# An encoder layer's last stage: finished output rows kept on chip and stored in four pieces per token tile, instead of three quarters parked in DRAM

## The chip, the cores and the metric

The kernel runs on one core of one Trainium2 chip. The metric is the device time of one execution in microseconds (us); less is better. The engines meant below are TensorE (PE in the profile, with its weight loads as PEld), VectorE (DVE), ScalarE (ACT), GpSimd (POOL) and SyncE (SP), whose queue issues nearly all transfers of this kernel.

## The reference

One encoder layer is applied to 512 + 256 = 768 tokens of width 2048. Only its end matters here:

```python
def mixer_layer(x, norm_g, w_in, conv_w, a_log, dt_bias, dn_gain, w_out):
    h = rms_norm(x, norm_g)
    proj = jnp.einsum('bsd,dp->bsp', h, w_in.astype(h.dtype)).astype(f32)
    ...
    mixed = jnp.concatenate([attn, dn], axis=-1).astype(x.dtype)
    return x + jnp.einsum('bsm,md->bsd', mixed, w_out.astype(x.dtype))

def encoder(...):
    x = mixer_layer(...)
    return rms_norm(x, final_norm_gain)     # y * rsqrt(mean(y*y) + eps) * gain, over all 2048 columns of a token
```

The final norm needs the sum of squares of a whole token row (2048 columns) before any column of it can be finished.

## The kernel before, in words

Everything is float32 in and out; each float32 operand of a product is split into a high and a low part, and three matmuls (high by high, high by low, low by high) make one product step. The projections, the attention heads and the DeltaNet heads come first; the mixed features (`mixD`) and several intermediates lie in DRAM.

The output projection is the last stage. It runs in two parts: part 0 takes the eight DeltaNet heads' features, part 1 the eight attention heads'. The features of part 0 are held in the tiles `xh0..xh7` and `xl0..xl7` of the pool `xp` (high and low part of one head, 128 x 768); those of part 1 in tiles `mh`/`ml` of the last pool `op`. Within a part the 2048 output columns are done in four quarters n = 0..3 of 512 columns (NQ = 4), and in a quarter the tokens in six tiles t = 0..5 of 128 (NT = 6). One token tile of one quarter is 8 heads x 3 = 24 matmuls of 512 columns into one PSUM bank `mmo`. (Where n is 0 the first three tiles are interleaved.) During the last token tile of a quarter `o_split` makes the weights of the next quarter: a load `st` of `w_out` arrives in one of five staging buffers, ACT casts the high part (`oh`), DVE or POOL subtracts (`ol`), and the buffer goes to a later load. These use the tiles `xh8..xh15`, `xl8..xl15`.

What is done with a finished bank is in three helpers. `o_fetch` asks for the other addend, a 128 x 512 tile `res` out of a ring of six (`wtile`): columns of `x` in part 0, the stored partial sum `yD` in part 1. `o_post` is called from `between` during the matmuls of the next token tile: DVE adds bank and `res`; in part 1 ACT then squares the sum with a running row sum (`sums`), and the sum is multiplied by the gain `fg` (on POOL in quarters 0 to 2, on DVE in quarter 3). `o_store` is called a little later and stores.

In part 1 the sums of quarters 0, 1 and 2 go from `res` to a DRAM buffer `zD`. In quarter 3 `o_fetch` also reads them back, into two tiles `row[0]` (columns 0 to 1023) and `row[1]` (1024 to 1535, its second half filled by the last quarter); the tag `row` has four buffers of 4 KB per partition, so two token tiles fit. After the last quarter's sum DVE and POOL make the row factor `r`, ACT multiplies `row[0]` by it and DVE `row[1]`, and both go to the output `y` as two 512 KB stores.

The order of instructions on each engine is the order in which the program is written; `drv` (a planner with costs) only decides where side tasks are woven in. All transfers named above are issued by SP in the order of the program: an issue that has to wait holds up all issues behind it. A buffer's next transfer waits until its earlier one is over.

Of the kernel before, what the change touches and what calls it, by code (L numbers as in the profile page):

```python
# [6 lines left out]
F32 = mybir.dt.float32  # L7
F32R = mybir.dt.float32r
AF = mybir.ActivationFunctionType
ALU = mybir.AluOpType  # L10
# [3 lines left out]
P = 128  # L14
D = 2048
NK = 16
T = 768
TP, TS = 512, 256
NT = T // P
# [48 lines left out]
class Driver:  # L68
# [88 lines left out]
    def spawn(self, gen, prio=0, bulk=False):  # L157
        self.n += 1
        self.tasks.append([self.end, prio, self.n, gen, bulk, None])
# [98 lines left out]
def encoder_kernel(tc, x, xT, wt, wab, wo, convw, gain, dngain, fgain, alog, dtb, cst, tabs, y):  # L258
# [3 lines left out]
    V, A, G = (Engine(drv, n, e) for n, e in (("V", nc.vector), ("A", nc.scalar), ("G", nc.gpsimd)))  # L262
    SY = DQ = Queue(drv, "Q", nc.sync)
    AQ = Queue(drv, "Q2", nc.scalar)
# [31 lines left out]
    yD = tc.dram_tile([NT, P, D], F32, name="yD")  # L296
    qD, kD, vD, agD = (tc.dram_tile([NH, P, T], F32, name=n) for n in ("qD", "kD", "vD", "agD"))
    gD = tc.dram_tile([NH, P, T], F32, name="gD")
    bD = tc.dram_tile([NK // 2, 2, P, HALF], F32, name="bD")
    zD = tc.dram_tile([NT, P, D], F32, name="zD")  # L300

    with (
        tc.manual_schedule(),
# [12 lines left out]
        def wtile(name):  # L316
            return drv.placed("w", wp.tile([P, 512], F32R, tag="w", name=name, bufs=6), 6)
# [29 lines left out]
        KB = 256  # L347
        TAGS, pool = {}, [None]

        def set_pool(p, tags):  # L350

            assert not any(drv.live.get(t, 0) for t in TAGS), drv.live
            pool[0] = p
            TAGS.clear()
            TAGS.update(tags)
            drv.most.update({t: n for t, (_, n) in TAGS.items()}, sa=2, sb=2, mm=4)
            for t in TAGS:
                drv.past.pop(t, None)
# [6 lines left out]
        if True:  # L365
            def st(tag, shape, name, dt=F32):

                n, bufs = TAGS[tag]
                t = drv.placed(tag, pool[0].tile([P, n], dt, tag=tag, name=name, bufs=bufs), bufs)
                v = t[:, :int(np.prod(shape))]  # L370
                if len(shape) == 2:
                    v = v.rearrange("p (a b) -> p a b", a=shape[0])
                elif len(shape) == 3:
                    v = v.rearrange("p (a b c) -> p a b c", a=shape[0], b=shape[1])
                return v
# [632 lines left out]
            def small(shape, tag, name, bufs=2):  # L1008
                return drv.placed(tag, pool[0].tile([P, *shape], F32, tag=tag, name=name, bufs=bufs), bufs)
# [515 lines left out]
            NQ = D // 512  # L1525
# [84 lines left out]
            def m_second():  # L1610
                for j in range(NH):
                    hi, lo = (pool[0].tile([P, T], F32R, name=f"m{w}{j}") for w in "hl")
                    mset[1][j] = (hi, lo)
                    SY.dma_start(lo.bitcast(F32), mixD[j])
                for j in range(NH):
                    yield lambda: drv.ready(mset[1][j][1])
                    m_split(1, j)
                    yield "early"
# [43 lines left out]
            late, outs, gains = {}, {}, {}  # L1662

            def open_last():

                global_close()
                op = op_cm.__enter__()
                set_pool(op, dict(row=(4 * KB, 4), fg=(2 * KB, 2)))
                late["sums"] = op.tile([P, NT, NQ], F32, name="sums")
                late["mhalf"] = op.tile([P, 1], F32, name="mhalf")  # L1670
                V.memset(late["mhalf"], -0.5)
                spawn(m_second(), -1)
                for n in (0, 1):
                    o_gain(n)
# [3 lines left out]
            def global_close():  # L1678
                give(*(t for t in list(TAGS) for _ in range(drv.live.get(t, 0))))
                heads[0].__exit__(None, None, None)  # L1680

            def o_gain(n):
                gains[n] = st("fg", (512,), f"fg{n}")
                SY.dma_start(gains[n], fgain[n * 512:(n + 1) * 512].partition_broadcast(P))

            def o_fetch(part, n, t):

                c = slice(n * 512, (n + 1) * 512)
                res = wtile(f"res{part}{n}_{t}").bitcast(F32)
                SY.dma_start(res, x[t * P:(t + 1) * P, c] if part == 0 else yD[t][:, c])  # L1690
                row = None
                if part and n == NQ - 1:
                    row = [st("row", (2, 512), f"row{t}_{h}") for h in (0, 1)]
                    SY.dma_start(row[0], zD[t][:, :1024].rearrange("p (a b) -> p a b", a=2))
                    SY.dma_start(row[1][:, 0], zD[t][:, 1024:1536])
                outs[part, n, t] = (res, row)

            def o_post(ps, part, n, t):
                res, row = outs[part, n, t]
                if part == 0:  # L1700
                    V.tensor_tensor(out=res, in0=ps, in1=res, op=ALU.add)
                    return
                yt = row[1][:, 1] if row else res
                V.tensor_tensor(out=yt, in0=ps, in1=res, op=ALU.add)
                A.activation(ps, yt, AF.Square, accum_out=late["sums"][:, t, n:n + 1])
                (V if row else G).tensor_tensor(out=yt, in0=yt, in1=gains[n], op=ALU.mult)
                if not row:
                    return
                r = small([2], "r", f"r{t}")
                V.tensor_reduce(out=r[:, 0:1], in_=late["sums"][:, t], axis=AX.X, op=ALU.add)  # L1710
                V.tensor_scalar(out=r[:, 0:1], in0=r[:, 0:1], scalar1=1.0 / D, scalar2=EPS, op0=ALU.mult, op1=ALU.add)
                G.tensor_tensor(out=r[:, 1:2], in0=r[:, 0:1], in1=late["mhalf"], op=ALU.pow)
                A.mul(row[0], row[0], r[:, 1:2])
                V.tensor_scalar(out=row[1], in0=row[1], scalar1=r[:, 1:2], scalar2=None, op0=ALU.mult)

            def o_store(part, n, t):
                res, row = outs.pop((part, n, t))
                if not row:
                    SY.dma_start((zD if part else yD)[t][:, n * 512:(n + 1) * 512], res)
                    return  # L1720
                for h in (1, 0):
                    SY.dma_start(y[t * P:(t + 1) * P, h * 1024:(h + 1) * 1024].rearrange("p (a b) -> p a b", a=2), row[h])

            pend, done = [], []

            def between(i):

# [7 lines left out]
            for part in (0, 1):  # L1735
                for n in range(NQ):
                    if part and not late:
                        drv.drain()
                        open_last()
# [3 lines left out]
                    if n == 0:  # L1743

                        group = 3
                        drv.until(lambda: free("mm", group))
                        ps3 = [bank(f"o{part}_{t}") for t in range(group)]
                        for j in range(NH):
                            drv.until(lambda: j in mdone[part] and wmade[0] > NH * NQ * part + j)
                            for t in range(group):  # L1750
                                ostep(ps3[t], part, t, j)
                                drv.slot()
                            between(j)
                        while pend:
                            between(1)
                            between(3)
                        o_fetch(part, 0, 0)
                        for t in range(group):
                            if t:
                                o_fetch(part, 0, t)  # L1760
                            pend.append((ps3[t], part, 0, t))
                    for t in range(group, NT):
                        if not late and not drv.tasks:
                            open_last()
                        ps = bank(f"o{part}{n}_{t}")
                        o_fetch(part, n, t)
                        for j in range(NH):
                            ostep(ps, part, t, j)
                            between(j)
                            if t == NT - 1 and j and (part, n) != (1, NQ - 1):  # L1770
                                o_split()
                            drv.slot()
                        if t == NT - 1 and (part, n) != (1, NQ - 1):
                            o_split()
                        pend.append((ps, part, n, t))
# [43 lines left out]
```

## Time and profile before

| | us |
|---|---|
| median of 3 runs | 1657.13 (1653.51 to 1657.84) |
| profiled execution, own time | 1661.15 |
| its span in the trace | 1659.4 |
| PE busy in the span | 1597.8 (96%) |
| mean granted TensorE clock | 0.985 of 2.4 GHz |

Times of rows are us from the start of the span. The profiled execution took 4.0 us longer than the median run, and 1.75 us of it lie outside the span. The profile's slices show PE at 0.9 or more in nearly all of the span, and at 0.5 in the last fortieth; that last stretch is where the rows below are from. A row of the timeline gives start, duration, engine (SPq is SP's queue), source line, operation, written and read tile, number of instructions merged, and in brackets how long the engine had been idle and who ended that.

### The profile page before, as it was taken

To read this page: it belongs to the slowest core of one execution; us is meant where nothing else is said; L and a number is where in the kernel's file an instruction comes from. 1 tells how busy PE (TensorE), PEld (TensorE's weight loads), DVE (VectorE), ACT (ScalarE), POOL (GpSimd) and SP (SyncE) were. 2 spreads that over 40 slices of the span, in tenths; PEclk is the share of its full clock that TensorE was granted. 3 is DMA by queue.
4 is the path that set the end of the run, shared out by engine and by line. 5 is a ranking of instruction groups with operands and counts; after the bars stand their busy time and mean duration, and the time that the engine had idled before them with its cause. 6 is when DMAs were issued, how large, how long until landed. Compare 5 with 4: busy or idle time off the path is not lost.

```text
span 1659.4 us, 30160 instructions
## 1 busy us (share of the span) xinstructions
PE 1597.8 (96%) x11675; PEld 1411.5 (85%) x11675; DVE 934.0 (56%) x2003; ACT 799.6 (48%) x1800; POOL 237.2 (14%) x233
## 2 busy tenths in 40 slices
PE   7998999999999999999999999999999889999995
PEld 6887999999888898988888888888878678887874
DVE  6558877778445554556555555665355555444332
ACT  6655333434354565556455656545355554433322
POOL 0000000000222221222213121312110011111220
PEclk9998999999999999999999999999999899999998
DMA  6232232323423323222223332232335455646557
GB/s 244 80 122 86 99 105 94 110 89 116 164 83 91 83 71 94 79 78 92 78 67 92 100 80 75 77 84 91 102 125 178 149 172 172 194 137 225 156 171 276
DMA packets 135265, 198.51 MB, mean 120 GB/s; under 512 B 49393, under 2 KB 60241, under 8 KB 135121
## 3 DMA queue, kind: packets, MB, share of 16 engines
q1 hardware_dynamic: 133968, 193.43, 36.2%
q10 hardware_dynamic: 1152, 3.15, 0.5%
q8 instruction: 92, 1.51, 0.4%
q14 instruction: 53, 0.43, 0.1%
HBM read 150.08 MB, written 46.45 MB: 118 GB/s over the span
## 4 chain that ended last, share of the span: by engine, by line
PE 80%; DMA 6%; DVE 5%; issue 4%; ACT 3%; POOL 1%; SPq 1%; ACTq 0%; DVEq 0%; POOLq 0%
PE mm L286 36%; PE mmo L286 8%; PE mmY L286 7%; PE mmr L286 7%; PE c L286 5%; PE mmX L286 5%; PE mmZ L286 5%; PE m L286 2%; DMA out_y<-row 2%; DMA st<-in_wo 1%; PE kk L286 1%; PE o L286 1%; DMA ak<-kD 1%; PE S L286 1%; DMA res<-in_x 1%
## 5 line engine op out<-in xcount | busy, mean ns | idle before, releaser
L286 PE MATMUL mm<-xl_x,hip 128*128 128x512 f32 (+1 forms) x1152 | 307.2, 348 | 0.0
L286 PE MATMUL mm<-xh_x,lop 128*128 128x512 f32 (+1 forms) x1152 | 305.5, 346 | 0.0
L286 PE MATMUL mm<-xh_x,hip 128*128 128x512 f32 (+1 forms) x1152 | 304.5, 345 | 0.0
L204 ACT CAST hip<-st 128x512 fp32r<-128x512 f32 x244 | 150.9, 619 | 236.8 <-PE mm L286 74.2
L204 POOL TENSOR_TENSOR lop<-st,hip 128x512 fp32r<-128x512 f32 x72 | 97.3, 1351 | 928.4 <-ACT hip L204 826.3
L204 DVE TENSOR_TENSOR lop<-st,hip 128x512 fp32r<-128x512 f32 x172 | 120.9, 703 | 193.8 <-ACT hip L204 188.6
L286 PEld LDWEIGHTS mm<-xh_x,hip 128*128 128x128 f32 x1152 | 176.5, 189 | 22.8
L286 PEld LDWEIGHTS mm<-xh_x,lop 128*128 128x128 f32 x1152 | 176.6, 189 | 21.7
L286 PEld LDWEIGHTS mm<-xl_x,hip 128*128 128x128 f32 x1152 | 176.4, 189 | 21.2
L286 PE MATMUL mmr<-xh_x,raw 128*128 128x512 f32 (+1 forms) x512 | 118.5, 345 | 11.3 <-ACT xh_x L204 9.6
L204 DVE SCALAR_TENSOR_TENSOR cacc<-cin,cw,cacc 128x772 f32<-128x772 f32 x96 | 107.4, 1119 | 23.4 <-ACT cacc L204 22.0
L204 ACT ACTIVATE s<-s,m 128x512 f32<-128x512 f32 (+1 forms) x96 | 61.5, 648 | 97.5 <-DVE m L204 97.4
L286 PEld LDWEIGHTS mmr<-xh_x,raw 128*128 128x128 f32 x512 | 79.7, 191 | 25.3 <-ACT xh_x L204 9.9
L286 PE MATMUL mmo<-oh,xh_m 128*128 128x512 f32 x192 | 79.2, 412 | 4.6 <-DVE q L204 4.1
L286 PE MATMUL mmo<-oh,mh 128*128 128x512 f32 x192 | 76.6, 399 | 1.8 <-ACT mh L204 1.6
L286 PE MATMUL mmo<-ol,xh_m 128*128 128x512 f32 x192 | 76.8, 400 | 1.0 <-POOL ol L204 0.5
L286 PE MATMUL mmo<-ol,mh 128*128 128x512 f32 x192 | 76.6, 399 | 0.6 <-DVE ol L204 0.5
L286 PE MATMUL mmo<-oh,ml 128*128 128x512 f32 x192 | 76.6, 399 | 0.3 <-DVE ml L204 0.3
L286 PE MATMUL mmo<-oh,xl_m 128*128 128x512 f32 x192 | 76.2, 397 | 0.0
L286 PE MATMUL mmr<-xl_x,raw 128*128 128x512 f32 (+1 forms) x256 | 67.0, 343 | 0.4 <-DVE xl_x L204 0.4
L204 ACT ACTIVATE z<-c,rho 128x128 f32<-128x128 f32 x96 | 35.1, 367 | 66.6 <-PE c L286 66.5
L204 DVE TENSOR_TENSOR res<-mmo,res 128x512 f32<-128x512 f32 x42 | 28.8, 687 | 67.5 <-PE mmo L286 46.3
(256 smaller groups left out, 3287.0 us busy)
## 6 DMA issues: line engine op xcount, KB each, us to landing
st<-in_wt SPq DMA_DIRECT2D x256, 256.0 KB
st<-in_wo SPq DMA_DIRECT2D x64, 256.0 KB
dec<-gcD SPq DMA_DIRECT2D x24, 256.0 KB
res<-in_x SPq DMA_DIRECT2D x24, 256.0 KB
yD<-res SPq DMA_DIRECT2D x24, 256.0 KB
res<-yD SPq DMA_DIRECT2D x24, 256.0 KB
out_y<-row SPq DMA_DIRECT2D x12, 512.0 KB
xst<-in_xT SPq DMA_DIRECT2D x15, 384.0 KB
```

Source lines behind the costliest of these rows:

```text
L204: r = f(*a, **k)
L286: r = PE.matmul(out, lhsT, rhs, start=start, stop=stop, skip_group_check=more)
```

## The change

The buffer `zD` is gone. In part 1 the sum of quarter n < 3 and token tile t is written by DVE not over `res` but to a place of its own, number i = 6n + t. The places 0 to 15 are the sixteen tiles `xh0`, `xl0`, `xh1`, ... `xl7` (their first 512 columns), which held the features of part 0; places 16 and 17 are tiles of the tag `row`, now two buffers of 2 KB. ACT squares it there and POOL multiplies it by the gain there. Nothing of it is stored until quarter 3, whose own sum stays in `res`. When the row factor of a token tile is there, ACT multiplies the pieces of quarters 0 and 2 and DVE those of quarters 1 and 3, and the four pieces go out as four stores of 256 KB, the third on ACT's queue, the others on SP's.

```diff
-    zD = tc.dram_tile([NT, P, D], F32, name="zD")
...
-                set_pool(op, dict(row=(4 * KB, 4), fg=(2 * KB, 2)))
+                set_pool(op, dict(row=(2 * KB, 2), fg=(2 * KB, 2)))
...
                 SY.dma_start(res, x[t * P:(t + 1) * P, c] if part == 0 else yD[t][:, c])
-                row = None
-                if part and n == NQ - 1:
-                    row = [st("row", (2, 512), f"row{t}_{h}") for h in (0, 1)]
-                    SY.dma_start(row[0], zD[t][:, :1024].rearrange("p (a b) -> p a b", a=2))
-                    SY.dma_start(row[1][:, 0], zD[t][:, 1024:1536])
-                outs[part, n, t] = (res, row)
+                dst = res
+                if part and n < NQ - 1:
+
+                    i = n * NT + t
+                    dst = st("row", (512,), f"row{i}")
+                    if i < NK:
+                        dst = xp.tile([P, T], F32R, tag=f"x{'hl'[i % 2]}{i // 2}", name=f"row{i}")[:, :512].bitcast(F32)
+                    kept[n, t] = dst
+                outs[part, n, t] = (res, dst)
...
-                yt = row[1][:, 1] if row else res
                 V.tensor_tensor(out=yt, in0=ps, in1=res, op=ALU.add)
                 A.activation(ps, yt, AF.Square, accum_out=late["sums"][:, t, n:n + 1])
-                (V if row else G).tensor_tensor(out=yt, in0=yt, in1=gains[n], op=ALU.mult)
-                if not row:
+                (G if n < NQ - 1 else V).tensor_tensor(out=yt, in0=yt, in1=gains[n], op=ALU.mult)
+                if n < NQ - 1:
                     return
...
-                A.mul(row[0], row[0], r[:, 1:2])
-                V.tensor_scalar(out=row[1], in0=row[1], scalar1=r[:, 1:2], scalar2=None, op0=ALU.mult)
+                kept[n, t] = yt
+                for i in range(NQ):
+                    if i % 2:
+                        V.tensor_scalar(out=kept[i, t], in0=kept[i, t], scalar1=r[:, 1:2], scalar2=None, op0=ALU.mult)
+                    else:
+                        A.mul(kept[i, t], kept[i, t], r[:, 1:2])
...
-                res, row = outs.pop((part, n, t))
-                if not row:
-                    SY.dma_start((zD if part else yD)[t][:, n * 512:(n + 1) * 512], res)
-                    return
-                for h in (1, 0):
-                    SY.dma_start(y[t * P:(t + 1) * P, h * 1024:(h + 1) * 1024].rearrange("p (a b) -> p a b", a=2), row[h])
+                res, _ = outs.pop((part, n, t))
+                if part == 0:
+                    SY.dma_start(yD[t][:, n * 512:(n + 1) * 512], res)
+                elif n == NQ - 1:
+                    for i in range(NQ):
+                        (AQ if i == 2 else SY).dma_start(y[t * P:(t + 1) * P, i * 512:(i + 1) * 512], kept.pop((i, t)))
```

The order of PE's instructions is the same in both programs. SP issues 24 transfers fewer (18 stores to `zD`, 12 loads from it, 12 stores to `out_y` go; 18 stores to `out_y` come), and ACT issues six more.

SP's queue at the end of the program before (names are `res13_4` for part 1, quarter 3, tile 4, and `row4_0`, `row4_1` for the two halves of tile 4's row):

```order
L248 DMA res13_4_17027<-yD_58 128x512
L248 DMA row4_0_17029<-zD_65 128x1024
L248 DMA row4_1_17030<-zD_65 128x512
L248 DMA out_y<-row3_1_16988 128x1024
L248 DMA out_y<-row3_0_16987 128x1024
L248 DMA res13_5_17069<-yD_58 128x512
L248 DMA row5_0_17071<-zD_65 128x1024
L248 DMA row5_1_17072<-zD_65 128x512
L248 DMA out_y<-row4_1_17030 128x1024
L248 DMA out_y<-row4_0_17029 128x1024
L248 DMA out_y<-row5_1_17072 128x1024
L248 DMA out_y<-row5_0_17071 128x1024
```

The same place in the changed program (`row3`, `row9` are the kept pieces of tile 3 from quarters 0 and 1; the piece of quarter 2 is on ACT's queue):

```order
L248 DMA out_y<-row2_16258 128x512
L248 DMA out_y<-row8_16477 128x512
L248 DMA out_y<-res13_2_16954 128x512
L248 DMA res13_4_17038<-yD_58 128x512
L248 DMA out_y<-row3_16263 128x512
L248 DMA out_y<-row9_16509 128x512
L248 DMA out_y<-res13_3_16996 128x512
L248 DMA res13_5_17080<-yD_58 128x512
L248 DMA out_y<-row4_16298 128x512
L248 DMA out_y<-row10_16541 128x512
L248 DMA out_y<-res13_4_17038 128x512
L248 DMA out_y<-row5_16333 128x512
```

No load of a row stands between a tile's stores and the next ones any more; the load `res13_5` still stands behind the stores of tile 3.

SP's queue where the weights of quarter 2 are loaded (`st309` to `st316`), before:

```order
L248 DMA zD_65<-res11_3_16497 128x512
L248 DMA res11_5_16559<-yD_58 128x512
L248 DMA st309_16574<-in_wo 128x512
L248 DMA st310_16583<-in_wo 128x512
L248 DMA zD_65<-res11_4_16528 128x512
L248 DMA st311_16593<-in_wo 128x512
L248 DMA st312_16602<-in_wo 128x512
```

And in the changed program:

```order
L248 DMA res11_4_16538<-yD_58 128x512
L248 DMA res11_5_16570<-yD_58 128x512
L248 DMA st309_16587<-in_wo 128x512
L248 DMA st310_16596<-in_wo 128x512
L248 DMA st311_16605<-in_wo 128x512
L248 DMA st312_16614<-in_wo 128x512
```

The store to `zD` between the second and the third weight load is gone; the quarters before and after this one show the same.

DVE's last instructions before, for token tile 5:

```order
L204 TENSOR_TENSOR row5_1_17072<-mmo13_5_17068,res13_5_17069 128x512
L204 TENSOR_TENSOR row5_1_17072<-row5_1_17072,fg3_16863 128x512
L204 TENSOR_REDUCE r5_17113<-sums_16018 128x1
L204 TENSOR_SCALAR r5_17113<-r5_17113 128x1
L204 TENSOR_SCALAR row5_1_17072<-row5_1_17072,r5_17113 128x1024
```

And in the changed program:

```order
L204 TENSOR_TENSOR res13_5_17080<-mmo13_5_17079,res13_5_17080 128x512
L204 TENSOR_TENSOR res13_5_17080<-res13_5_17080,fg3_16879 128x512
L204 TENSOR_REDUCE r5_17124<-sums_16017 128x1
L204 TENSOR_SCALAR r5_17124<-r5_17124 128x1
L204 TENSOR_SCALAR row11_16573<-row11_16573,r5_17124 128x512
L204 TENSOR_SCALAR res13_5_17080<-res13_5_17080,r5_17124 128x512
```

The chain from the bank to the row factor is the same; the product over 1024 columns has become two of 512, and ACT's likewise.

## Rows read from the trace of the kernel before

**Rows 1.** The page's first line, and two stretches of the last 60 us.

```profile
span 1659.4 us, 30160 instructions
...
1600.00:1640.00 40.00, 39.78 (x171) 31.69 (x170) 16.65 (x30) 13.42 (x24) 4.79 (x6) 1.00 0.71 241
1640.00:1659.40 19.40, 1.70 (x8) 1.03 (x6) 4.72 (x10) 3.74 (x6) 1.08 (x2) 0.60 0.74 262
```

**Rows 2.** The chain that ended last, from 1595 us: shares, and its longest pieces.

```profile
by line: DMA out_y<-row 41.4%; PE mmo L286 10.8%; DMA res<-yD 9.2%; DMA row<-zD 8.3%; issue 5.1%; SPq L248 4.7%; DVE row L204 4.6%; DVE ol L204 2.5%; ACT mmo L204 1.1%; DVE res L204 1.1%; ACT oh L204 1.0%; POOL r L204 0.9%; DVE r L204 0.4%;
...
1618.39 7.59 DMA out_y<-row
...
1648.02 5.36 DMA row<-zD
```

**Rows 3.** Timeline of SP's queue, last tiles.

```profile
1634.18 0.76 SPq L248 DMA_DIRECT2D res<-yD  x1
1639.82 1.57 SPq L248 DMA_DIRECT2D row<-zD  x2
1641.50 0.84 SPq L248 DMA_DIRECT2D out_y<-row  x2
1642.39 0.98 SPq L248 DMA_DIRECT2D res<-yD  x1
```

**Rows 4.** Timeline of PE at the three quarter boundaries, and PE's last matmul.

```profile
1543.98 0.40 PE L286 MATMUL mmo<-oh,mh 128*128 128x512 f32 x1
...
1544.84 0.39 PE L286 MATMUL mmo<-oh,ml 128*128 128x512 f32 x1
...
1577.60 0.39 PE L286 MATMUL mmo<-oh,ml 128*128 128x512 f32 x1
...
1578.89 0.51 PE L286 MATMUL mmo<-ol,mh 128*128 128x512 f32 x1 [0.23 <-DVE ol L204]
1579.23 0.39 PE L286 MATMUL mmo<-oh,ml 128*128 128x512 f32 x1
...
1612.00 0.40 PE L286 MATMUL mmo<-oh,ml 128*128 128x512 f32 x1
...
1613.30 0.40 PE L286 MATMUL mmo<-oh,ml 128*128 128x512 f32 x1
...
1641.30 0.40 PE L286 MATMUL mmo<-oh,ml 128*128 128x512 f32 x1
```

**Rows 5.** Timeline of SP and ACT at the second boundary.

```profile
1572.13 0.38 SPq L248 DMA_DIRECT2D zD<-res  x1
1572.61 6.58 SPq L248 DMA_DIRECT2D st<-in_wo  x6
...
1577.49 0.62 ACT L204 CAST oh<-st 128x512 fp32r<-128x512 f32 x1 [2.46 <-DMA st<-in_wo]
```

**Rows 6.** Timeline of DVE and ACT in quarter 3 and after the last matmul.

```profile
1613.96 0.69 DVE L204 TENSOR_TENSOR row<-mmo,res 128x512 f32<-128x512 f32 x1 [0.45 <-DMA res<-yD]
...
1641.79 0.69 DVE L204 TENSOR_TENSOR row<-mmo,res 128x512 f32<-128x512 f32 x1 [2.50 <-PE mmo L286]
...
1648.76 0.69 DVE L204 TENSOR_TENSOR row<-mmo,res 128x512 f32<-128x512 f32 x1 [2.40 <-DMA res<-yD]
...
1653.48 0.75 DVE L204 TENSOR_SCALAR row<-row,r 128x1024 f32<-128x1024 f32 x1 [2.24 <-DMA row<-zD]
...
1642.58 0.60 ACT L204 ACTIVATE mmo<-row 128x512 f32<-128x512 f32 x1 [3.53 <-DVE row L204]
...
1645.00 1.15 ACT L204 ACTIVATE row<-row,r 128x1024 f32<-128x1024 f32 x1 [1.70 <-POOL r L204]
```

**Rows 7.** Stretches: the transfers of the last stores, and one of quarter 3 under PE.

```profile
1655.30:1657.30 2.00, 0.00 (x0) 0.00 (x0) 0.00 (x0) 0.00 (x0) 0.00 (x0) 0.50 1.02 410
1657.30:1658.30 1.00, 0.00 (x0) 0.00 (x0) 0.00 (x0) 0.00 (x0) 0.00 (x0) 0.50 0.41 160
...
1630.00:1640.00 10.00, 10.00 (x45) 8.04 (x44) 3.11 (x6) 3.02 (x4) 0.54 (x1) 1.00 0.85 292
```

The columns of a stretch are its length, the busy time of PE, PEld, DVE, ACT and POOL with the number of instructions, the granted clock, the busy share of the DMA engines and GB/s.

More of the change, by code (lines that the diff above doesn't have):

```diff
@@ L1690, in o_fetch @@
                 SY.dma_start(res, x[t * P:(t + 1) * P, c] if part == 0 else yD[t][:, c])
-                row = None
-                if part and n == NQ - 1:
-                    row = [st("row", (2, 512), f"row{t}_{h}") for h in (0, 1)]
-                    SY.dma_start(row[0], zD[t][:, :1024].rearrange("p (a b) -> p a b", a=2))
-                    SY.dma_start(row[1][:, 0], zD[t][:, 1024:1536])
-                outs[part, n, t] = (res, row)
+                dst = res
[6 more added lines that the diff above has]
+                outs[part, n, t] = (res, dst)
             def o_post(ps, part, n, t):
-                res, row = outs[part, n, t]
+                res, yt = outs[part, n, t]
                 if part == 0:
@@ L1712, in o_post @@
                 G.tensor_tensor(out=r[:, 1:2], in0=r[:, 0:1], in1=late["mhalf"], op=ALU.pow)
-                A.mul(row[0], row[0], r[:, 1:2])
-                V.tensor_scalar(out=row[1], in0=row[1], scalar1=r[:, 1:2], scalar2=None, op0=ALU.mult)
-            def o_store(part, n, t):
-                res, row = outs.pop((part, n, t))
-                if not row:
-                    SY.dma_start((zD if part else yD)[t][:, n * 512:(n + 1) * 512], res)
-                    return
-                for h in (1, 0):
-                    SY.dma_start(y[t * P:(t + 1) * P, h * 1024:(h + 1) * 1024].rearrange("p (a b) -> p a b", a=2), row[h])
-            pend, done = [], []
+                kept[n, t] = yt
[4 more added lines that the diff above has]
+                        A.mul(kept[i, t], kept[i, t], r[:, 1:2])
+            def o_store(part, n, t):
+                res, _ = outs.pop((part, n, t))
[4 more added lines that the diff above has]
+                        (AQ if i == 2 else SY).dma_start(y[t * P:(t + 1) * P, i * 512:(i + 1) * 512], kept.pop((i, t)))
+            pend, done, kept = [], [], {}
             def between(i):
```

## The prediction

> **What bounds the kernel now.** I read the page first: PE is busy in 96% of the span, so a change at the end can only win what lies outside PE's work. The table of stretches shows where that is: from 1600 to 1640 us PE works 39.78 of 40 us, and from 1640 to the end only 1.70 of 19.40, at a lower granted clock, while the DMA engines stay 0.74 busy [rows 1]. Then the chain that ended last, from 1595 us on: 41% of it is stores to the output and 8% reads from `zD`, and only 11% matmuls [rows 2]. So in the last quarter the kernel is paced by a loop of transfers. SP's queue shows the loop: a tile's row loads wait until the stores of two tiles earlier have landed, because only two tiles fit into the `row` buffers; the next stores and the next `res` stand behind those loads in SP's order [rows 3]. PE has left the loop behind. Its last matmul ends at 1641.30 + 0.40 = 1641.70, and DVE starts the add of the last tile only at 1648.76, when its `res` has landed; the product by the row factor then waits for `row` until 1653.48 [rows 4, 6]. From PE's end to the end of the span pass 17.7 us.
>
> PE also has three short stalls in part 1, one at each quarter boundary. Matmuls start (1641.30 - 1613.30) / 120 = 0.233 us apart, 120 being the five tiles of 24 between these two rows. Across the boundaries 1543.98 to 1544.84 is two steps in 0.86 (0.39 too long), 1577.60 to 1579.23 three steps in 1.63 (0.93 too long), 1612.00 to 1613.30 three steps in 1.30 (0.60 too long): 1.92 us in all [rows 4]. They wait for a split of weights, whose cast waited 2.46 us for a load that SP issued behind a store to `zD` [rows 5].
>
> **The change, part by part.**
> 1. The adds to kept places, quarters 0 to 2. Same DVE add, same square, same POOL product, other addresses. The places are free: the matmuls that read part 0's features stand before part 1's on PE, and the add waits for a bank of part 1 in any case. I take 0; a `res` buffer comes free after the add and not after a store, so `res` loads go out earlier, which is cover and no cost.
> 2. 18 stores to `zD` removed. In quarters 0 to 2 they lie under PE, but one stands between the second and the third weight load of each boundary. It takes SP's slot from 1572.13 to 1572.61, 0.48 us, and 256 KB of wire ahead of the late load; at 292 GB/s [rows 7] these are 0.9 us. The late load should land about 1.4 us earlier, more than the largest stall of 0.93. I take all three stalls away: PE ends at 1641.70 - 1.92 = 1639.78. Bounds: 0 if something else makes the loads late, 1.92 at most.
> 3. 12 loads from `zD` removed: 768 KB per tile, and with them the wait for the stores of two tiles before. Per tile SP and ACT now issue one `res` and four stores, 1.25 MB in place of 2 MB. At 292 GB/s [rows 7] 1.31e6 bytes take 4.5 us, below PE's 24 x 0.233 = 5.6 us per tile, so PE should pace the last quarter.
> 4. What is late next: `res` of tile t + 2 stands behind the stores of tile t. The stores follow PE's end of tile t by 3.30 us (to the products, below), 0.62 for ACT's first product, then three SP issues of 0.42: `res` is issued 5.3 us after that end, and needed 11.2 us after it. It has 5.9 us. Before, `res` took 7.6 us (1634.18 to 1641.79) and 6.4 us (1642.39 to 1648.76) from issue to the add, with 1.75 MB of row loads and stores ahead of it [rows 3, 6]. (The row of the first add names PE as releaser; but PE had ended that tile one tile, 5.6 us, before, so I read it as `res`.) With 1 MB ahead it is 0.79e6 bytes less, 2.7 us at 292 GB/s: 3.7 to 4.9 us. I take in time, with 1 us to spare; the bound is 7.6.
> 5. From PE's end to the row factor. The clean example is tile 4's chain, whose add starts 0.09 us after PE's end and whose ACT product starts at 1645.00: 3.30 us after 1641.70 [rows 4, 6]. It is the same instructions in the changed kernel, so 1639.78 + 3.30 = 1643.08.
> 6. The products. ACT's over 1024 columns takes 1.15 and a 512-column pass 0.60 [rows 6]; two of 512 cost little more than one of 1024. The first store can go out after the first piece, 0.62 us later, and 0.05 for the semaphore: 1643.75. The others follow 0.42 us apart, and ACT issues its own about when SP issues its last.
> 7. The drain. Before, DVE's last product ended at 1653.48 + 0.75 = 1654.23, and the span ended at 1659.40: 5.17 us for issue, 1 MB at about 410 GB/s and landing [rows 1, 6, 7]. The data are the same 1 MB, in rows of 2 KB and not 4 KB. Bounds: the same 5.2 us, or 1.05 MB at 292 GB/s, 1.0 us more. I take 5.2, because these stores too have the wires for themselves: the stores of tile 4 were issued 5.6 us earlier. The end is 1643.75 + 5.2 = 1648.95.
>
> Sum against the profiled execution: 1659.4 - 1648.95 = 10.4 us less, of which 1.9 are PE's stalls and 8.5 the tail. The median of the runs lies 4.0 us below the profiled execution's own time (1661.15 against 1657.13); taking the 10.4 us from the median gives 1646.7. If the profiled run's extra 4.0 us lay all in the tail that I remove, the gain would be 6.4 us, and that is why the range goes further up than down.
>
> On step 7 the Trainium skill has a rule against this change: "DMA: Bandwidth & Descriptors", Anatomy of one DMA and Rules for kernel authors, gives a transfer about 2.0 us fixed plus its bytes at 436 GB/s (fitted on GpSimd's path) and wants small ones merged. By that, one after the other, four of 256 KB would be 10.4 us and two of 512 KB 6.4, an estimate of 4 us more. The trace speaks against adding them up: the two last stores moved their bytes at 410 GB/s with the DMA engines fully busy for 2 us on end [rows 7], so the fixed part was paid once.
>
> **The rivals.**
> - The stalls stay (step 2 fails): the weights are late for want of free staging buffers and not because of the store. For it: five buffers, six issues spread over 6.58 us [rows 5]. Against it: the load that is late is the one behind the store. The gain is then 8.5 us: 1648.6.
> - `res` is late (step 4 fails): if a `res` still takes 7.6 us it is 1.7 us late at tile 3, tile 5's is issued as much later, and the last add comes 3.4 us late. The gain is 7.0 us: 1650.1.
> - Every piece pays its own fixed time in the drain. The last data move at about 1657.3 + 0.4 = 1657.7 [rows 7], 1.7 us before the end. If each store went only after the landing of the one before, the drain would be four times 1.7 plus 0.64 of data each, and 0.9 before the first data (5.17 less 1.7, less 2.6 for 1 MB): 10.3 us and not 5.2, so 1651.8, just at the edge of a measurable gain. The unbroken 410 GB/s [rows 7] leaves it little. This is what the Trainium skill's rule would come to here.
> - Within 0.3%: the tail is slower only under the profiler, and `res` is late as well: 6.4 - 3.4 = 3.0 us, 1654.1.
> - Slower: SP is paced by landings. A tile still has five transfers on eight completion counters, so each issue waits for the transfer eight places before, 1.6 tiles back. This is nothing while a landing takes under 1.6 x 5.6 = 9.0 us; it costs if the stores, twice as many, land slower. To lose 5 us a landing would have to take about 13 us (pace 5/8 x 13 = 8.1 us per tile, against (1648.76 - 1613.96) / 5 = 7.0 before, as DVE's adds of tiles 0 and 5 stand). The longest in the chain is 7.59 with more bytes in flight [rows 2], so I give it little. Price: 1662.
>
> That the change does not do what it says I exclude: the loop of waits through `zD` is gone from SP's order.
>
> **How the numbers follow.** 0.3% is 5.0 us, about what a measurement of this kernel can tell from no change. Chances: the forecast 0.60, stalls stay 0.12, `res` late 0.14, each piece pays 0.04, within 0.3% 0.07, slower 0.03. Faster is then 0.60 + 0.12 + 0.14 + 0.04 = 0.90. The forecast is 1646.7. The range reaches up past the late `res` and the 6.4 us gain (1650.7) to 1651.0, and down to 1644.0, since single runs of before lie up to 3.6 us under their median. Outside it are above all the last three cases and part of the spread.
>
> **What would show it.** Right: PE's matmuls stay 0.233 us apart over the three boundaries; the add of tile 5 is released by PE, 0.1 us after its last matmul; about 9.2 us from PE's end to the end of the span; no wait of SP for a landing of `out_y` until the end. Wrong in step 2: the boundary rows still show an `oh` or `ol` as releaser. Wrong in step 4: the last adds are released by `res`. Wrong in step 7: the drain shows gaps, or well under 410 GB/s. The prediction as a whole fails if unprofiled runs have no such tail, or if moving the `res` loads forward makes them collide with weight loads and lengthens the boundary stalls.

## The result

| | before | changed |
|---|---|---|
| median, us | 1657.47 (1653.51 to 1657.84) | 1647.09 (1644.38 to 1647.82) |
| profiled execution: own time; span | 1661.15; 1659.4 | 1644.38; 1642.7 |
| PE's last matmul to the end of the span | 17.7 | 9.0 |
| stalls at the three quarter boundaries | 1.92 | none |

Medians are of four runs each. The ratio is 0.9938 with a 95% interval of 0.9925 to 0.995: 10.4 us faster, as forecast (1646.7). The two profiled spans differ by more, 16.7 us, and that needs sorting out before anything else is read from them.

First the end. Stretches of the changed kernel's last quarter, the columns as in [rows 7]; they answer to [rows 1]:

```profile
1600.00:1633.60 33.60, 33.60 (x145) 26.94 (x143) 15.61 (x35) 12.89 (x25) 4.03 (x6) 1.00 0.61 205
1633.60:1642.70 9.10, 0.03 (x1) 0.00 (x0) 2.49 (x6) 2.06 (x4) 0.54 (x1) 0.75 0.53 200
```

PE works without a break to 1633.6, the DMA engines are less busy under it (0.61 for 0.71), and 9.1 us follow in place of 17.7. The chain that ended last, from 1580 us on, its shares and its first piece; it answers to [rows 2]:

```profile
by line: PE mmo L286 85.2%; DVE res L204 2.2%; issue 1.3%; ACT mmo L204 1.2%; ACT row L204 1.2%; POOLq L1819 0.9%; DVE r L204 0.4%; POOLq L204 0.1%
18 pieces in order of time: start us, us, what
1579.96 53.69 PE mmo L286 x231
```

No transfer is left in it: 54 us of matmuls in one piece, then the arithmetic of the last tile. (The chain ends with the last engine instruction, at 1638.2, so the drain of the last stores is not in it.) The timeline of the last tile on PE, DVE, ACT and SP answers to [rows 3, 6]:

```profile
1633.25 0.39 PE L286 MATMUL mmo<-oh,ml 128*128 128x512 f32 x1
...
1633.67 0.69 DVE L204 TENSOR_TENSOR res<-mmo,res 128x512 f32<-128x512 f32 x1 [1.51 <-PE mmo L286]
...
1636.85 1.33 ACT L204 ACTIVATE row<-row,r 128x512 f32<-128x512 f32 x2 [1.73 <-POOL r L204]
...
1628.21 0.65 SPq L248 DMA_DIRECT2D res<-yD  x1
1632.03 0.81 SPq L248 DMA_DIRECT2D out_y<-row  x2
1632.93 0.40 SPq L248 DMA_DIRECT2D out_y<-res  x1
1637.60 0.81 SPq L248 DMA_DIRECT2D out_y<-row  x2
1638.50 0.41 SPq L248 DMA_DIRECT2D out_y<-res  x1
```

The add is released by PE and no longer by `res`: the `res` of tile 5 was issued at 1628.21, 5.5 us before its use. From PE's end (1633.64) to the products are 3.2 us, to the first store 4.0, and from there to the end of the span 5.1. In the drain, the stretch that answers to [rows 7]:

```profile
1639.00:1641.00 2.00, 0.00 (x0) 0.00 (x0) 0.00 (x0) 0.00 (x0) 0.00 (x0) 0.50 1.02 383
```

Four stores in rows of 2 KB keep the DMA engines as full as the two in rows of 4 KB did, at 383 GB/s instead of 410.

PE across the second boundary, answering to [rows 4]:

```profile
1571.21 0.39 PE L286 MATMUL mmo<-oh,ml 128*128 128x512 f32 x1
...
1571.90 0.40 PE L286 MATMUL mmo<-oh,ml 128*128 128x512 f32 x1
```

Three steps take 0.69 us where they took 1.63: the stall is gone in this execution.

The rest of the 16.7 us lies before the change acts. SP's first skipped transfer would have been issued at about 1524 us. The first matmul of part 1 starts at 1501.73 in the profile before and at 1497.30 in that of the changed kernel, 4.4 us apart, with the same program up to there. So the sum for this pair is 4.4 from the start, 8.7 from the end (17.73 less 9.02), 1.9 to 2.1 from the boundaries (by the two measures given below), and the last 1.6 from the first quarter of part 1, nearly all of it a spell of lower clock, told at the end. The profile before was of a long execution and the profile after of a short one; further profiles below tell what belongs to the kernels.

### The profile page after: what moved, and what is told of

Read it like the earlier page. It is cut to its first block, busy times and chain, and to the rows that moved or that the text cites. A ratio compares the mean times of both kernels' runs of the same rounds, so it can differ in the third digit from the quotient of the medians.

```text
span 1642.7 us, 30109 instructions
## 1 busy us (share of the span) xinstructions
PE 1590.2 (97%) x11675; PEld 1407.4 (86%) x11675; DVE 934.4 (57%) x2009; ACT 800.4 (49%) x1806; POOL 236.1 (14%) x233
## 4 chain that ended last, share of the span: by engine, by line
PE 83%; DVE 5%; DMA 4%; ACT 3%; issue 3%; SPq 1%; POOL 1%; ACTq 0%; POOLq 0%; DVEq 0%
PE mm L286 36%; PE mmo L286 11%; PE mmY L286 7%; PE mmr L286 6%; PE c L286 5%; PE mmZ L286 5%; PE mmX L286 5%; PE m L286 2%; DMA xst<-in_xT 1%; PE kk L286 1%; PE o L286 1%; PE S L286 1%; DMA ak<-kD 1%; SPq L248 1%; DMA res<-in_x 1%
## 5 line engine op out<-in xcount | busy, mean ns | idle before, releaser
L204 DVE TENSOR_TENSOR ol<-st,oh 128x512 fp32r<-128x512 f32 x52 | 42.7, 845 | 26.6 <-ACT oh L204 26.4
```

The source lines that it names most:

```text
L204: r = f(*a, **k)
```

## The experiments

For each kernel three numbers of its profile are given. The tail is the span less the end of PE's last matmul. A boundary stall is the time from the first matmul of a quarter of part 1 to the first of the next (in the last quarter to its last) less so many steps of 0.2322 us, close to the pace of the changed kernel's last quarter (143 steps in 33.23 us). By this measure the first profile before has 2.13 us in quarters 1 to 3 (1.92 from the rows at the boundaries alone). The start is that of part 1's first matmul.

| kernel | start | stalls | tail | median, us |
|---|---|---|---|---|
| before, first profile | 1501.7 | 0.43 + 0.95 + 0.75 | 17.73 | 1657.47 |
| before, second (e9) | 1496.8 | 0.71 + 0.75 + 0.47 | 17.73 | 1659.36 |
| changed, first | 1497.3 | 0.02 + 0.03 + 0.02 | 9.02 | 1647.09 |
| changed, e1 | 1500.9 | 0.03 + 0.67 + 0.60 | 9.02 | 1647.17 |
| changed, e10 | 1501.6 | 0.02 + 0.67 + 0.02 | 9.03 | 1649.09 |
| dead stores, e2 | 1496.6 | 1.38 + 0.91 + 0.68 | 9.20 | 1649.04 |
| dead stores, e11 | 1500.0 | 0.55 + 0.87 + 1.22 | 9.19 | 1650.56 |
| round trip, no loop, e3 | 1495.3 | 0.27 + 3.83 + 1.27 | 11.77 | 1651.77 |
| eight stores, e4 | 1497.9 | 0.03 + 0.03 + 0.05 | 11.32 | 1649.65 |
| all stores on SP, e5 | 1496.4 | 0.21 + 0.05 + 0.03 | 9.07 | 1648.10 |
| before, stores moved, e6 | 1499.6 | 0.02 + 0.51 + 1.03 | 18.47 | 1656.30 |
| shorter end, e7 | 1500.6 | 0.02 + 0.62 + 0.03 | 8.49 | 1649.10 |
| weights a quarter ahead, e8 | 1497.2 | 0.16 + 0.16 + 0.16 | 9.02 | 1645.22 |
| both, e12 | 1498.9 | 0.03 + 0.03 + 0.02 | 8.50 | 1647.74 |

e1 to e4 stand beside runs of before with a median of 1657.45, e5 to e8 beside 1657.95, e9 to e12 beside 1659.36. Medians are compared within such a group; in the two rows of before the last column is the median of the runs of before that belong to the profile's group.

**The changed kernel again (e1, e10) and the kernel before again (e9).** No edit.

> The changed kernel once more, beside fresh runs of before. My theory puts the gain into two places, the quarter boundaries of part 1 (1.9 us) and the time from PE's last matmul to the end of the span (17.7 us before, 9.1 in the profile after); so a second profile must show the same 9.1 within 0.3 us and boundaries without excess, while the point in time where part 1 begins may move by several us from one execution to the next. The rival, that some of the 16.7 us between the two profiled spans comes from the change acting earlier, expects the start of part 1 to stay as early as in the first profile after, near 1497.6 us, and never to come near the 1502.2 of before.

> The changed kernel a third time, beside the two kernels below on the same chip. Tail 9.0 us; boundaries between 0.1 and 1.3 us in all.

> The kernel before, profiled a second time, to see which of its numbers repeat. My theory: the tail again 17 to 18.5 us from PE's last matmul to the end; the three boundaries with 1.5 us or more of stall in all; the start of part 1 anywhere between 1496 and 1502 us, as in the other executions. The rival, that the first profile was an odd one, expects a tail below 15 us or boundaries below 1 us.

The ratios are 0.9938 (0.9914 to 0.9962) and 0.9937 (0.9921 to 0.9953), like the first. The tail repeats to 0.02 us in either kernel, so 8.7 us of the gain are a property of the kernel. The start of part 1 moves by 4 to 5 us in either kernel without regard to the change, as does the whole of what lies before it; the rival of e1 has fallen. But the boundaries of the changed kernel are not always clean, against what was expected of e1: it has 1.3 us there, e10 0.7. A weight load can be late without any store. PE's waits in part 1 of e1 (engine and tile, then total, times and longest), and at its second boundary the timeline of SP and ACT and two stretches:

```profile
PE mmo L286 <- DVE ol L204: 0.4, 2, 0.2
...
1568.19 7.88 SPq L248 DMA_DIRECT2D st<-in_wo  x8
...
1574.37 0.62 ACT L204 CAST oh<-st 128x512 fp32r<-128x512 f32 x1 [2.23 <-DMA st<-in_wo]
...
1568.00:1570.00 2.00, 2.00 (x10) 1.62 (x9) 2.00 (x5) 0.84 (x2) 0.00 (x0) 1.00 0.34 105
1570.00:1574.00 4.00, 4.00 (x19) 3.26 (x18) 1.96 (x3) 1.24 (x2) 0.00 (x0) 1.00 0.90 303
```

The cast at 1574.37 is that of the third load of the eight. With five staging buffers only three of a quarter's eight weights are loaded at its boundary; the other five of this burst are for the quarter after it. (So in SP's queue as listed with the change `st309` to `st311` are the last three weights of quarter 2, and `st312` to `st316` the first five of quarter 3.) By 1574 the stretches have moved 2 x 105 + 4 x 303 = 1422 KB, over five loads of 262 KB, and yet the third was not there. The loads did not overtake each other: the trace has sixteen completion marks for a transfer, and counted by the last of them the third landed at 1574.30, the fourth at 1574.97 and the fifth at 1575.63. But fifteen of the third's sixteen marks were there by 1572.93, and one came 1.4 us after them.

The landing of this third load sets the stall. In the twelve profiles whose weights are loaded at the boundary (all but e8 and e12) there are 36 boundaries. At 35 of them PE stalls (counted by its long steps there) by as much as the third load lands later than 3.53 us after the quarter's first matmul, to within 0.05 us, and not at all when it lands earlier; at the other one (the second of e3) the granted clock fell as well. In the six profiles with the changed kernel's loads and no `zD` (the first, e1, e10, e4, e5, e7) the third load lands 2.4 to 4.2 us after that matmul, 3.3 on average over 18 boundaries, so some are late by themselves.

At the second boundary of these six the record shows something that goes with it: a 16 KB packet in the DMA queue for instructions, taking 0.9 to 1.3 us. Where it began 0.8 to 1.0 us after the quarter's first matmul (the first, e4, e5) the third load landed at 3.5 us and nothing stalled; where it began 1.3 to 1.8 us after it (e1, e10, e7) the load landed at 4.1 to 4.2 and PE lost 0.6 to 0.7. That the packet holds up the last of the sixteen parts is not shown, since the trace does not tell on which DMA engine it ran; the third boundary of e1, where all sixteen marks came late (the fifteenth at 3.95 us), has another cause that stays open.

**Dead stores to `zD` (e2, e11).** The stores of quarters 0 to 2 are put back on SP's queue where they stood; nothing reads them.

```diff
                 if part == 0:
                     SY.dma_start(yD[t][:, n * 512:(n + 1) * 512], res)
+                elif n < NQ - 1:
+                    SY.dma_start(zD[t][:, n * 512:(n + 1) * 512], kept[n, t])
```

> The changed kernel, with the 18 stores to zD put back on SP's queue where they stood; nothing reads them. My theory: the three boundary stalls come back, 0.4 + 0.9 + 0.6 us as before (1.9 in all), because the store stands between weight loads; the tail from PE's last matmul to the end stays at 9.1 us. About 2 us over the changed kernel. Rival, that the stalls came from the early or late `res` loads or from the addresses of the sums: no stall comes back, same time as the changed kernel.

> The changed kernel with the dead stores to zD once more. If they make the weight loads late, the boundaries show 2 to 3 us again, as in their first profile, and the median stands 1 to 3 us above the changed kernel's in the same call. If that first profile was chance, boundaries of 0 to 1.3 us and the same median.

Both profiles have stalls at all three boundaries, 2.97 and 2.64 us in all, more than the 1.9 expected, against 0.07, 1.30 and 0.71 in the changed kernel; the tail stays at 9.2. The medians are 1.9 and 1.5 us above the changed kernel's in the same groups (ratios to before 0.9953, 0.9935 to 0.997, and 0.995, 0.9938 to 0.9962; the intervals overlap with the changed kernel's). PE's waits in part 1 of e11:

```profile
PE mmo L286 <- DVE ol L204: 0.7, 3, 0.2
PE mmo L286 <- ACT oh L204: 0.3, 1, 0.3
```

The changed kernel's first profile has no such row. So the stores make the weight loads late, as step 2 had it. By the landings, the third load comes 4.3 us after the quarter's first matmul on average over the twelve boundaries of the kernel before (two profiles) and of e2 and e11, 0.9 later than the 3.3 without the stores.

**Stores moved behind the weight loads, in the kernel before (e6).**

```diff
-                if i % 4 == 3 and done:
+                if i % 4 == 3 and done and not (part and n < NQ - 1 and t == NT - 1):
```

(In the interleaved first group `t` is set to 0 ahead of `between`.)

> The kernel before, with the stores to zD that stood between the weight loads of a boundary moved behind them; everything else as before. If the stores made the weight loads late (my step 2), the second and third boundary lose most of their 0.9 and 0.6 us of stall and the first its 0.4, and the kernel gains up to 1.9 us with the tail at 17 to 18 us. The rival, that a weight load is late by itself in some executions (the changed kernel's second profile had 0.67 and 0.60 us of stall without any such store), expects stalls between 0 and 1.3 us in all, of the same sizes as in the changed kernel's two profiles, and a time that cannot be told from before.

1656.30 against 1657.95, ratio 0.9994 (0.9983 to 1.0005): not to be told from before. The first boundary is clean, the third is not: 1.03 us. Step 2 is right that the store does harm there, and too simple: in this profile the third loads still land at 3.24, 4.01 and 4.43 us, and moving the stores buys half a microsecond of the 2 us. The tail of 18.47 shows that nothing else of the gain comes from here.

**Round trip kept, loop removed (e3).** The sums go to `zD` as before, and quarter 3 reads them back into twelve places of 768 columns in part 0's features, so no load waits for a place. Three stores per tile, all on SP.

```diff
+                if part and n == NQ - 1:
+                    for h in (0, 1):
+                        kept[h, t] = xp.tile([P, T], F32R, tag=f"x{'hl'[h]}{t}", name=f"row{t}_{h}").bitcast(F32)
+                        SY.dma_start(kept[h, t], zD[t][:, h * T:(h + 1) * T])
+                outs[part, n, t] = (res, res)
```

> The round trip through zD kept, with all its bytes, but read back into twelve places of 768 columns in part 0's features, so that no load has to wait for a place; three stores per tile. My theory says that the loop of landings was the cause, and that without it the tail shrinks to 9.1 us plus what the wires cannot carry: 2 MB per tile at 292 to 410 GB/s are 5.1 to 7.2 us against PE's 5.6, so the last tile is at most some 3 us late: 9 to 12.5 us of tail, and the boundary stalls of 1.9 us stay. The rival, that the bytes of the round trip and not the waits were what paced the last quarter, expects nearly the whole tail of before: 15 us or more.

The tail is 11.77 us, inside the 9 to 12.5 of the theory and far from the rival's 15. In the kernel before, SP's waits from 1605 us on (releaser, total, times, longest) are led by

```profile
SPq L248 <- DMA out_y<-row: 20.2, 8, 5.1
```

In e3 the same wait from 1603 us on, the last add, and the stretch of quarter 3:

```profile
SPq L248 <- DMA out_y<-row: 0.4, 1, 0.4
...
1641.66 0.69 DVE L204 TENSOR_TENSOR res<-mmo,res 128x512 f32<-128x512 f32 x1 [2.79 <-issue]
...
1604.00:1638.00 34.00, 33.42 (x142) 26.39 (x141) 15.23 (x34) 10.12 (x20) 4.02 (x6) 1.00 0.88 310
```

SP waits 0.4 us for a landing of a store where it waited 20.2; those waits were the loop of [rows 2, 3]. The last add starts 3.0 us after PE's end (1638.66). Its row names no transfer, but its `res`, issued at 1634.67, landed at 1641.58 by its completion marks. So of the 8.71 us of tail the loop is 5.96 (17.73 less 11.77), and 2.75 (11.77 less 9.02) stay with the bytes of the round trip. That it is the rate of the wires which makes this `res` late is argued from the DMA engines' 0.88 at 310 GB/s; no run varies it alone. The median, 1651.77, is 4.6 above the changed kernel's: 2.75 from the tail, the rest from the boundaries, which are worse here than the 1.9 us expected: 5.4 in this profile, 3.8 of it at the second, where the third load landed at 5.67 us and the granted clock then fell (0.78 over 1575 to 1580).

**Eight stores per tile (e4).** Each piece is cut into two stores of 64 partitions.

```diff
+                        for h in (0, 64):
+                            (AQ if i == 2 else SY).dma_start(y[t * P + h:t * P + h + 64, i * 512:(i + 1) * 512], k[h:h + 64])
```

> The changed kernel with every piece cut into two stores of 64 partitions, so eight stores of 128 KB per token tile and nine transfers per tile on eight completion counters. My theory: the bytes flow without a break and only the issues cost, so the drain grows by the SP issues added after the first piece, at most three more of 0.42 us beyond what the wires need: 0 to 1 us, no slip under PE, since a landing takes well under a tile's 5.6 us. Rival one, that each store pays a fixed time in turn: 4 x 1.7 us or more longer. Rival two, that SP is paced by landings once a tile has more transfers than counters: PE is not slowed, but the last adds come late, several us on the tail.

The tail grows by 2.3 us, more than the theory's 1 and less than either rival's. Timeline of DVE, ACT and SP at the end (PE ends at 1636.16), and the drain:

```profile
1636.97 0.69 DVE L204 TENSOR_TENSOR res<-mmo,res 128x512 f32<-128x512 f32 x1 [0.82 <-DMA res<-yD]
...
1636.63 1.13 ACTq L248 DMA_DIRECT2D out_y<-row  x2
1637.80 0.60 ACT L204 ACTIVATE mmo<-res 128x512 f32<-128x512 f32 x1 [1.20 <-DVE res L204]
...
1636.01 2.66 SPq L248 DMA_DIRECT2D out_y<-row  x4
1638.77 1.18 SPq L248 DMA_DIRECT2D out_y<-res  x2
...
1642.00:1646.00 4.00, 0.00 (x0) 0.00 (x0) 0.00 (x0) 0.00 (x0) 0.00 (x0) 0.50 0.89 261
```

A store of 64 partitions takes SP about 0.6 us to issue, not 0.4, so a tile's six on SP are 3.9 us, and the `res` behind them is issued late: the last add starts 0.8 us after PE's end. ACT's own issues of tile 4 hold back the square of tile 5 by 0.1 us, and the drain, at 261 GB/s, is 1.4 us longer. SP begins the drain's issues at 1641.00 and the last of them at 1644.09, 3.1 us apart, where the changed kernel had 0.9. By their completion marks the first store of the drain landed 2.2 us after its issue began and the last 2.4 (2.1 and 3.2 in the changed kernel), so no backlog of transfers had built up behind the issues. Neither a fixed time for each store in turn nor the completion counters show (SP waits for no landing from 1605 us to the program's end); what costs is the queue's issue time.

**All stores on SP (e5).**

```diff
-                        (AQ if i == 2 else SY).dma_start(
+                        SY.dma_start(
```

> The changed kernel with all four stores of a tile on SP's queue. My theory: SP issues one more transfer of 0.4 us per tile, still ahead of need, and the drain is set by the wires once it has begun; tail 9.0 to 9.5 us, same time as the changed kernel within the spread. Rival, that ACT's queue was what took the load off SP and kept `res` in time: adds released by `res` again, tail 1 us or more longer.

Tail 9.07, inside the 9.0 to 9.5; 1648.10 against 1657.95, ratio 0.9947 (0.9929 to 0.9965). ACT's queue plays no part in the gain.

**Shorter end (e7).** The row sum and its power come ahead of the last gain product, and the stores go in the order in which the pieces are finished.

```diff
+                if n < NQ - 1:
+                    G.tensor_tensor(out=yt, in0=yt, in1=gains[n], op=ALU.mult)
+                    return
...
                 G.tensor_tensor(out=r[:, 1:2], in0=r[:, 0:1], in1=late["mhalf"], op=ALU.pow)
+                V.tensor_tensor(out=yt, in0=yt, in1=gains[n], op=ALU.mult)
...
-                    for i in range(NQ):
+                    for i in (1, 0, 3, 2):
```

> The changed kernel with the row sum and its power ahead of the last gain product on DVE (so the product runs beside the power on GpSimd) and the stores in the order in which the pieces are finished. The product of 0.69 us and the 0.25 us that the first store waits for ACT's first piece leave the path: tail 9.0 - 0.6 to 0.9 = 8.1 to 8.4 us. Rival, that the drain is what counts and the path before it hides behind other work: tail still 9.0.

Tail 8.49, 0.5 us less, short of the 0.6 to 0.9. The power on POOL, in the changed kernel and in this one:

```profile
1636.27 0.54 POOL L204 TENSOR_TENSOR r<-r,mhalf 128x1 f32<-128x1 f32 x1 [5.03 <-DVE r L204]
```

```profile
1641.46 0.83 POOL L204 TENSOR_TENSOR r<-r,mhalf 128x1 f32<-128x1 f32 x1 [4.75 <-DVE r L204]
```

Beside DVE's product it takes 0.83 us and not 0.54, and it ends only after the product does. Half a microsecond is below what the median can show.

**Weights a quarter ahead (e8), and both (e12).** Eight staging buffers in the last pool hold the weights of the next quarter, asked for a quarter ahead (in the program's order at tile 3 of quarter 0 and at tile 1 of quarters 1 and 2).

```diff
+                    if n >= cur["far"]:
+                        if n >= cur["go"]:
+                            return
+                        stages[n] = st("wst8", (512,), f"st{n}")
...
+                        if part and n < NQ - 1 and t == max(group, 1):
+                            cur["go"] = ob + (n + 6) * NH
+                            feed()
```

> The changed kernel with eight staging buffers of their own for the weights of quarters 1 to 3, loaded a quarter ahead, so that no weight load falls into a boundary. If late weight loads are what stalls the boundaries, whatever makes them late, the three boundaries have no excess (under 0.1 us each) in every profile, and the kernel gains the mean of what the changed kernel loses there, 0 to 1.3 us. If the stalls come from something else (ACT or DVE being late), 0.6 us stalls stay.

> The changed kernel with both the shorter end (row sum ahead of the gain product, stores in the order of the pieces) and the weights of quarters 1 to 3 loaded a quarter ahead. Tail 8.5 us as with the first alone, boundaries 0.5 us or less as with the second alone; the median 1 to 2 us under the changed kernel's. If the two get in each other's way, not below it.

No stall is left in either profile: e12 has 0.02 to 0.03 per quarter; e8's 0.16 is a matmul pace of 0.2333 throughout the quarter, with no step above 0.24, and no stall. ACT's eight casts at a boundary of e12 are one unbroken group, where e1 waited for single loads:

```profile
1565.94 4.78 ACT L204 CAST oh<-st 128x512 fp32r<-128x512 f32 x8
```

Six clean boundaries alone could be chance, since 13 of the 18 above are clean within 0.05 us too; together with the landings, which account for each stall, they show that the boundary stalls were late weight loads. e8 comes to 1645.22 against 1657.95 (0.9926, 0.9908 to 0.9943), e12 to 1647.74 (0.993, 0.9916 to 0.9943) beside the changed kernel's 1649.09. Both medians are the lowest of their groups, by 1.4 us for e12 over the changed kernel, but the intervals overlap: a likely gain that these runs do not prove.

## Why the prediction held

Total: 10.4 us forecast, 10.4 measured. By steps:

- Step 1 (adds to kept places cost nothing): right. In the first profile quarters 1 to 3 run on PE with 0.07 us lost in all.
- Step 2 (1.92 us of stalls go): the cause was right and the size was off. The first profile shows all of it gone, which is the best case; over the three profiles of the changed kernel 0.7 us are left on average (0.07, 1.30, 0.71), against 2.0 in the two of before (2.13, 1.93), so the term is about 1.3. The step took the late load to land about 1.4 us earlier and set that against the largest stall; it comes 0.9 us earlier on average, and what was missed is that its landing varies by 1.8 us from boundary to boundary without any store, so that taking the store away makes a late load rarer but does not exclude it. The rival that the stalls stay, for want of free staging buffers, is wrong in its forecast (e2, e11: the store matters) and partly right in its cause: with eight buffers (e8, e12) the rest of the stalls is gone.
- Steps 3 and 4 (PE paces the last quarter, `res` is in time): right. In every profile of the changed kernel the adds of the last quarter's tiles 1 to 5 are released by PE. In its three profiles the loads of `res` for tiles 2 to 5 landed, by their completion marks, 3.9 to 4.7 us after their issue, inside the 3.7 to 4.9 worked out. In e4, where the issues take longer, the adds of tiles 2 to 5 did wait for `res`, used 3.3 to 4.2 us after its issue.
- Steps 5 to 7 (3.30, then 0.67, then 5.2 us): 3.2, 0.75 and 5.1. The drain in rows of 2 KB ran at 383 GB/s, near the upper of the two rates that bounded it.
- The sum of the parts that belong to the kernels is 8.7 + 1.3 = 10.0 us; the medians gave 10.4, with a spread of single runs of 3 to 8 us. That forecast and median agree to a tenth is luck: the tail gave 0.2 more than the 8.5 forecast, the boundaries 0.6 less than their 1.9, and the rest is spread of what lies before.
- The worry that the profiled execution's extra 4.0 us lie in the tail was unfounded: the tail was 17.73 in a profiled execution of 1661.15 and in one of 1656.12. The difference lies before part 1 and was 4.9 us at its first matmul.
- Each piece paying its own fixed time, and SP paced by landings: neither happened, and e4, with twice as many stores, shows neither. The Trainium skill's rule ("DMA: Bandwidth & Descriptors", Rules for kernel authors), that small transfers be merged, does have a side that the forecast undervalued: in e4 halving the stores once more cost 2.3 us. In this trace the price came through SP's issue time and not through a fixed time per store in turn.

The loop of waits was the greater part of the tail, but not all: e3 splits it into 5.96 us of waiting for places and 2.75 us that stay as long as the bytes do.

## What to carry to other kernels

When a chain ends in transfers, look for the load that waits for a buffer that a store must first leave: it ties the pace to a landing, 5.1 to 7.6 us for the stores of tiles 0 to 4 here, and not to bytes, and places that earlier stages have left can break it even if the bytes stay (6.0 of 8.7 us here). Compare two kernels by stages counted from a point that both share, and profile each more than once: here the two spans differed by 16.7 us, of which 10 were the change. A weight load that is asked for only at the boundary where it is used may or may not land in time from one execution to the next; asked for one stage ahead, none was late in the two profiles taken.

## What was not expected of the hardware

- About 6 us after the start of part 1 PE stalls for some 2 us; the row of the matmul that ends the stall, in the changed kernel's first profile, names ACT's cast of part 1's features (`mh`):

```profile
1505.27 0.50 PE L286 MATMUL mmo<-oh,mh 128*128 128x512 f32 x1 [1.53 <-ACT mh L204]
```

  In some executions the granted clock then falls to 0.66 on average over 5 us, part of that time at the lower level of 1.2 GHz, in others it stays at 1.00. The stretch after the stall in the changed kernel's first profile and in e10:

```profile
1505.00:1510.00 5.00, 4.47 (x18) 3.38 (x19) 4.96 (x7) 3.16 (x5) 0.00 (x0) 1.00 0.78 252
```

```profile
1510.00:1515.00 5.00, 4.75 (x14) 3.40 (x14) 4.81 (x6) 2.68 (x4) 0.00 (x0) 0.66 0.78 238
```

  By the measure of the stalls above, the first quarter has 2.3 to 2.6 us too much without the fall and 3.9 to 4.5 with it, so a fall goes with about 1.7 us, some 0.2 of it a longer stall. Ten of the fourteen profiles had it: both of the kernel before, and e2, e3, e4, e6, e7, e10, e11 and e12. The changed kernel's first, e1, e5 and e8 had not. What PE did before it differs: from the start of the last matmul ahead of the stall to the start of the next one 1.88 to 1.93 us passed in the changed kernel's first, e1 and e8 and 2.20 in e5, and 2.04 to 2.54 in the ten with the fall. Why e5 has none stays open. The edits act only after this point, but for e8 and e12, which move weight loads away from it (one had the fall and one not); it is part of the spread.
- Beside a product on DVE over 512 columns a power on POOL over one column took 0.82 to 0.93 us and not 0.54 to 0.56, in all six tiles of e7 and again of e12.
- A store of 64 partitions took the issuing queue about 0.6 us, one of 128 partitions with the same row length 0.4 (e4).
